# Attention: values of heads 0 to 3 as plain fp32 products of copied weights and values instead of three products of rounded and low parts

## The chip, the cores and the metric

The kernel runs on one core of one Trainium2 chip. The metric is the device time of an execution in microseconds (us). A core has a matrix engine (TensorE, in profiles PE for the products and PEld for the loads of their stationary operand), three engines for elementwise work (VectorE or DVE, ScalarE or ACT, GpSimd or POOL) and SyncE (SP), which issues the DMA transfers here. Operands of TensorE lie in SBUF, its results in PSUM. Each engine works through its own list of instructions in order and waits on semaphores for the others.

## The reference

The reference is a small diffusion transformer of two layers, in fp32: 256 latent and 256 context tokens of width 1024. Each layer has a half feed-forward block, a mixer, and another half feed-forward block, each with its modulation, residual and layer norm. The mixer of the first layer is attention with 8 query heads on 2 key-value heads of width 128; that of the second is an mLSTM. What the change touches is the attention's softmax and its product with the values:

```python
def gqa_softmax(q, k, v):
    s = jnp.einsum('bqhgd,bkhd->bhgqk', q, k).astype(jnp.float32) * (ATT_HEAD_DIM ** -0.5)
    p = jax.nn.softmax(s, axis=-1).astype(v.dtype)
    return jnp.einsum('bhgqk,bkhd->bqhgd', p, v)
...
    ob = lax.map(lambda qblk: gqa_softmax(qblk, k_all, v_all), qb)
...
        oc = gqa_softmax(qc.reshape(B, Lc, ATT_KV_HEADS, ATT_GROUP, ATT_HEAD_DIM), kc, vc)
```

Latent queries see all 512 tokens, context queries the 256 context tokens. Heads 0 to 3 use key-value head 0, heads 4 to 7 key-value head 1.

## The kernel before

All activations stand transposed in SBUF: 8 tiles of 128 features by 512 tokens, the latent tokens in columns 0 to 255, the context in 256 to 511. A product of fp32 operands is made as three products of type fp32r: `split` (L224) writes a rounded copy `h` with ScalarE (L225) and the low part `x - h` with VectorE (L230), and `mm3` (L239) adds up high × high, high × low and low × high in PSUM (all three on L241). Weights come in chunks of 128×1024 through `raw` (L204, the DMA on SyncE) and are split likewise.

Attention (L947) first makes keys, values and queries: `part` makes one token tile (128 tokens) of one block of 256 columns with `token_product` (L935, products on L941 to L943); `evac` (L971) takes the results out of PSUM, `turn` (L990) transposes queries and keys on TensorE (L998) and applies the rotation. For block 0, `evac` splits the values (L978) into `vt`, a rounded and a low tile of 4 token tiles × 2 key-value heads × 128.

Then the loop of L1143 runs over 24 steps, head by head, three steps `i` a head. Steps 0 and 1 are the two blocks of 128 latent queries against all 512 tokens, step 2 holds both blocks of context queries against the 256 context tokens. `scores` (L1024) makes the 128×512 scores in three rounded products, or six of half the width in step 2, and its softmax: minimum (the scores are negated) on VectorE (L1036), exponential with its sum on ScalarE (L1039), reciprocal (L1043), scaling (L1049, on POOL for step 0, on VectorE else). Three steps later (`AHEAD`) `values` (L1052) transposes the weights on TensorE (L1056) into one of two PSUM tiles (`ps`, L200), and splits that tile: steps 0 and 1 into the halves of `pT` (L1064), step 2 into `pC` (L1066). In step 2 it then makes the head's output: four groups of three rounded products for the latent columns (L1068) and two groups for the context columns (L1072), each 128×256. The output is split into the input of the out projection (L1078), or for head 0, while a projection still uses that place, copied to `qT` (L1080). `queries` (L1019) splits the next head's queries.

Between these stand the projections that are left (`rest`, L1132), the loads of the output weights (`OUTAT`), and from step 20 on the first half of the out projection (`mix_unit`, L1158). The order of the instructions of each engine isn't the order of the code: a list scheduler sets it from its own costs, unless an instruction is held in program order by `pin` (the transposes are, L998 and L1056).

Of the kernel before, what the change touches and what calls it, by code (L numbers as in the profile page):

```python
# [9 lines left out]
F32 = mybir.dt.float32  # L10
F32R = mybir.dt.float32r
# [7 lines left out]
P = 128  # L19
D = 1024  # L20
ND = D // P
T = 512
TL = 256
# [8 lines left out]
BLOCK = 64  # L32

SH = 16
SHM = 48
# [137 lines left out]
class Body:  # L173
# [12 lines left out]
    def t(self, shape, dt=F32, tag=None, bufs=None, pool=None):  # L186
        self.n += 1
        kw = {"bufs": bufs} if bufs else {}
        return (pool or self.sp).tile(list(shape), dt, name=f"t{self.n}", tag=tag or f"u{self.n}", **kw)
# [757 lines left out]
    def attention(self, gate, side):  # L947
        nc, V, S, a = self.nc, self.nc.vector, self.nc.scalar, self.a
        with self.tc.tile_pool(name="att", bufs=1) as gp:
            t = lambda shape, dt=F32, **k: self.t(shape, dt, pool=gp, **k)  # L950
# [5 lines left out]
            for tab, g in zip(tabs, (gq, gk)):  # L956
                S.activation(tab, tabs[1], AF.Copy, scale=g)
            qT = t([P, HEADS, T])
            kT, vt = ([t(shape, F32R) for _ in range(2)] for shape in ([P, 2, T], [P, 4, 2, P]))
            acc, ws = {}, {}  # L960

            def part(blk, tt, step=lambda k: None, ks=range(ND)):
# [8 lines left out]
            def evac(blk, tts):  # L971

                n = 4 if blk else 2
                ss = self.small(len(tts) * n)
                os = [acc[blk, tt].rearrange("p (n f) -> p n f", f=P) for tt in tts]
                for j, (tt, o) in enumerate(zip(tts, os)):
                    if not blk:
                        self.split(o[:, 2:4, :], vt[0][:, tt], vt[1][:, tt])  # L978
                    sq = self.tmp(n * P).rearrange("p (n f) -> p n f", f=P)
                    S.activation(sq, o[:, :n, :], AF.Square)  # L980
                    V.tensor_reduce(ss[:, j * n : (j + 1) * n], sq, AX.X, ALU.add)
                r = self.rsqrt(ss, len(tts) * n, RMS_EPS, 1.0 / P)
                qs = [t([P, n, P], tag="qn", bufs=3) for _ in tts]
                for i in range(n):
                    for j, (q, o) in enumerate(zip(qs, os)):
                        S.activation(q[:, i, :], o[:, i, :], AF.Copy, scale=r[:, j * n + i : j * n + i + 1])
                m = 4 // len(tts)
                return [lambda i=i: turn(blk, tts, i, min(m, n - i), qs) for i in range(0, n, m)]
# [63 lines left out]
            def values(hd, i, e, pt):  # L1052
                kv = hd // 4
                tp = self.ps()
                for k in range(4):
                    self.pin(nc.tensor.transpose(tp[:, k * P : (k + 1) * P], e[:, k * P : (k + 1) * P], self.ident))  # L1056
                if i == 0:
                    pt[:] = [
                        [x.rearrange("p (k q f) -> p k q f", k=4, q=2) for x in self.pair(sh=SHM)],
                        [t([P, 4 * P + BLOCK], F32R, tag=k, bufs=2)[:, SHM : SHM + 4 * P].rearrange("p (k q f) -> p k q f", k=2, q=2) for k in ("ph", "pl")],  # L1060
                    ]
                pT, pC = pt
                if i < 2:
                    self.split(tp.rearrange("p (k f) -> p k f", f=P), *(x[:, :, i, :] for x in pT))  # L1064
                    return
                self.split(tp.rearrange("p (q k f) -> p k q f", q=2, k=2), *pC)  # L1066
                o = self.mm()
                for k in range(4):  # L1068
                    self.mm3(
                        o[:, 0:TL], [x[:, k, kv, :] for x in vt], [x[:, k].rearrange("p q f -> p (q f)") for x in pT], k == 0, k == 3  # L1070
                    )
                for k in range(2):  # L1072
                    self.mm3(
                        o[:, TL:T], [x[:, 2 + k, kv, :] for x in vt], [x[:, k].rearrange("p q f -> p (q f)") for x in pC],
                        k == 0, k == 1,
                    )
                if (2, 3) in acc:
                    self.split(o, self.xh[:, hd, :T], self.xl[:, hd, :T])  # L1078
                else:
                    S.copy(qT[:, hd, :], o)  # L1080
                    kept.append(hd)
# [9 lines left out]
            def done(n, blk, tts, lag=LAG):  # L1091
                wait.extend((n + lag + i, f) for i, f in enumerate(evac(blk, tts)))

            n = 0
# [47 lines left out]
            es, pt = [], []  # L1142
            for n in range(max(len(subs) + AHEAD, MIXAT + ND)):  # L1143
                if n < len(subs):
                    hd, i = subs[n]
# [623 lines left out]
```

## Time and profile before

| what | value |
|---|---|
| time, median of 3 runs | 1627.38 us (1626.02 to 1630.14) |
| span of the profiled execution, first to last instruction | 1625.5 us |
| mean granted TensorE clock | 0.997 |
| attention heads, start of the first and of the last transpose of weights | 451.3 and 525.3 us |
| bytes by DMA, mean rate | 251.56 MB, 155 GB/s |

The span is the only time recorded of the profiled execution itself; it lies 1.9 us under the median. Times in the timeline are counted from the start of the span. A group's line gives line, engine, operation, output and inputs, shapes, count, then busy time, mean duration in ns, and the idle time of the engine ahead of these instructions with what ended it. In the timeline a row has start and duration in us, engine, line, operation, shapes and count of merged instructions, and in brackets the idle time of that engine before it, with the instruction that ended it. PE shows a plain fp32 product as two records. A matmul's shown duration is longer than the distance to the next one, since matmuls are pipelined; the distance between starts is what one costs.

### The profile page before, as it was taken

The page shows a single profiled execution, that of the slowest core. Times are in us where ns is not written, and L with a number is a line of the kernel's source. Part 1 is how long each engine was busy: PE and PEld are TensorE (multiplying, and loading weights), DVE is VectorE, ACT ScalarE, POOL GpSimd, SP SyncE. Part 2 cuts the span into 40 slices and gives each one's busy share as a digit, 9 for nine tenths or more (in the row PEclk, how much of TensorE's full clock was granted, in tenths as well). Part 3 has the DMA queues.
Part 4 walks back from the last instruction along what each step waited for, and adds up shares of the span by engine and source line. Part 5 has one row for each costly group of instructions (what it writes and reads, how often), then busy time and mean ns, then how long its engine had stood idle before and what let it go on. Part 6 is the DMA issues. An engine that isn't in the chain of part 4 may idle for free. (4 is left out here: it accounts for less than half of the span.)

```text
span 1625.5 us, 26587 instructions
## 1 busy us (share of the span) xinstructions
PE 1606.9 (99%) x10304; PEld 1451.7 (89%) x10304; DVE 1355.7 (83%) x2699; ACT 749.2 (46%) x1272; POOL 63.0 (4%) x77
## 2 busy tenths in 40 slices
PE   9999999999999999999999999999999999999998
PEld 7888888889988998889998998889999989999987
DVE  7899977649889879899986879699966968897687
ACT  6522132314676443316652444336652657566542
POOL 0000000001011100000000100000001000030000
PEclk9999999999999999999999999999999999999999
DMA  9687766422202447633445258713363343437552
GB/s 358 221 252 237 235 205 187 137 66 85 66 1 80 151 134 221 219 117 105 129 146 180 79 165 289 253 58 118 104 225 100 98 130 87 142 110 253 181 176 91
DMA packets 72222, 251.56 MB, mean 155 GB/s; under 512 B 7960, under 2 KB 10776, under 8 KB 72096
## 3 DMA queue, kind: packets, MB, share of 16 engines
q1 hardware_dynamic: 71520, 249.09, 47.7%
q8 instruction: 80, 1.31, 0.3%
q10 hardware_dynamic: 576, 0.79, 0.1%
q14 instruction: 46, 0.38, 0.1%
HBM read 248.79 MB, written 1.05 MB: 154 GB/s over the span
## 5 line engine op out<-in xcount | busy, mean ns | idle before, releaser
L241 PE MATMUL t<-t,t 128*128 128x256 f32 (+2 forms) x8412 | 1317.0, 318 | 6.4 <-ACT t L225 3.3
L241 PEld LDWEIGHTS t<-t,t 128*128 128x128 f32 x8412 | 1185.7, 188 | 125.4 <-ACT t L225 4.7
L225 ACT CAST t<-t 128x1024 fp32r<-128x1024 f32 (+3 forms) x521 | 428.5, 844 | 485.8 <-PE t L241 214.5
L230 DVE TENSOR_TENSOR t<-t,t 128x256 fp32r<-128x256 f32 (+2 forms) x740 | 513.8, 729 | 111.9 <-ACT t L225 107.7
L350 DVE SCALAR_TENSOR_TENSOR t<-t,t 128x1024 bf16<-128x1024 f32 x224 | 260.7, 1220 | 0.0
L588 ACT ACTIVATE t<-t 128x512 f32<-128x512 f32 (+1 forms) x71 | 34.5, 490 | 103.5 <-PE t L241 102.4
L941 PE MATMUL t<-t,t 128*128 128x256 f32 (+1 forms) x256 | 79.3, 310 | 0.0
L718 DVE SCALAR_TENSOR_TENSOR t<-t,t,t 128x256 f32<-128x256 f32 x96 | 42.7, 478 | 43.9 <-PE t L241 43.7
L943 PE MATMUL t<-t,t 128*128 128x256 f32 (+1 forms) x256 | 78.4, 306 | 0.0
L942 PE MATMUL t<-t,t 128*128 128x256 f32 (+1 forms) x256 | 78.4, 306 | 0.0
L589 DVE TENSOR_TENSOR t<-t,t 128x512 f32<-128x512 f32 (+1 forms) x71 | 39.0, 553 | 40.6 <-PE t L241 28.1
L484 POOL TENSOR_TENSOR t<-t,t 128x256 f32<-128x256 f32 x30 | 23.4, 781 | 1104.9 <-ACT t L474 1103.5
L869 PE MATMUL t<-t,t 128*128 128x512 f32 (+1 forms) x300 | 60.5, 364 | 0.0
L869 PEld LDWEIGHTS t<-t,t 128*128 128x128 f32 x300 | 51.5, 189 | 8.9
L474 ACT ACTIVATE t<-t 128x256 f32<-128x256 f32 x72 | 26.1, 412 | 65.5 <-DVE t L467 65.5
L1456 PE MATMUL t<-t,t 128*128 128x512 f32 (+2 forms) x276 | 55.6, 356 | 0.0
L1456 PEld LDWEIGHTS t<-t,t 128*128 128x128 f32 (+1 forms) x276 | 44.9, 183 | 10.9 <-issue 0.9
L942 PEld LDWEIGHTS t<-t,t 128*128 128x128 f32 x256 | 48.1, 188 | 3.0 <-DVE t L230 0.5
L941 PEld LDWEIGHTS t<-t,t 128*128 128x128 f32 x256 | 48.3, 189 | 2.7
L943 PEld LDWEIGHTS t<-t,t 128*128 128x128 f32 x256 | 48.1, 188 | 2.5
L541 ACT ACTIVATE t<-t,t 128x256 fp32r<-128x256 f32 x72 | 32.8, 503 | 30.1 <-DVE t L540 30.1
L641 DVE TENSOR_TENSOR t<-t,t 128x512 f32<-128x512 f32 x66 | 45.2, 685 | 0.4
(206 smaller groups left out, 1078.6 us busy)
## 6 DMA issues: line engine op xcount, KB each, us to landing
t<-in_ffn_in SPq DMA_DIRECT2D x168, 512.0 KB, 4.1
t<-in_ada_w SPq DMA_DIRECT2D x138, 512.0 KB, 4.4
t<-in_ffn_out SPq DMA_DIRECT2D x66, 512.0 KB, 4.5
t<-in_ffn_last SPq DMA_DIRECT2D x22, 512.0 KB, 3.5
t<-in_att_in SPq DMA_DIRECT2D x12, 512.0 KB, 3.5
t<-in_att_out SPq DMA_DIRECT2D x8, 512.0 KB, 3.6
t<-in_ml_qk SPq DMA_DIRECT2D x8, 512.0 KB, 3.6
t<-in_ml_v SPq DMA_DIRECT2D x8, 512.0 KB, 3.5
```

What stands on the lines that cost most here:

```text
L225: self.behind(self.nc.scalar.copy(h, x))
L230: self.behind(self.nc.vector.tensor_tensor(out=ls, in0=xs, in1=hs.bitcast(F32), op=ALU.subtract))
L241: mm = lambda *k, **kw: self.nc.tensor.matmul(*k, skip_group_check=not group, **kw)
L350: ins = nc.vector.scalar_tensor_tensor(self.tmp().bitcast(BF16), r, 1.0, self.cb[:, v, :], ALU.mult, ALU.mult, accum_out=to)
L589: V.tensor_tensor(out=sl, in0=sl, in1=pu[:, :n], op=ALU.mult)
L641: add = lambda o, x, y: V.tensor_tensor(out=o, in0=x, in1=y, op=ALU.add)
L718: V.scalar_tensor_tensor(z, y[:, gg[0] - t0 : gg[1] - t0], gate()[:, v, d : d + 1], z, ALU.mult, ALU.add)
L869: pin(nc.tensor.matmul(o, gs[g], ws[k][w][:, i : i + n], start=k == k0 and g == w == 0, stop=k == k1 - 1 and g == 1,))
L941: mm(o, self.xh[:, k, c], wh, start=k == 0, stop=False)
L942: mm(o, self.xh[:, k, c], wl, start=False, stop=False)
L943: mm(o, self.xl[:, k, c], wh, start=False, stop=k == ND - 1)
L1456: mm = lambda *k, **kw: pin(nc.tensor.matmul(*k, **kw))
```

## The change

Only attention is changed. For key-value head 0, `evac` copies the values unrounded into `vf`, and `values` copies the transposed weights unrounded (on ScalarE, into a buffer of the same ring `w`, without the offset of 48 columns, and for the context into a new tile `pf` with two buffers) and makes one plain fp32 product for each group of three. `vt` keeps key-value head 1 alone. For heads 4 to 7 the computation is that of before.

```diff
-            kT, vt = ([t(shape, F32R) for _ in range(2)] for shape in ([P, 2, T], [P, 4, 2, P]))
+            kT, vt = ([t(shape, F32R) for _ in range(2)] for shape in ([P, 2, T], [P, 4, P]))
+            vf = t([P, 4, P])
...
                     if not blk:
-                        self.split(o[:, 2:4, :], vt[0][:, tt], vt[1][:, tt])
+                        S.copy(vf[:, tt], o[:, 2, :])
+                        self.split(o[:, 3, :], vt[0][:, tt], vt[1][:, tt])
...
+                if not kv:
+                    if i == 0:
+                        x, y = self.pair(F32)[0], t([P, 4 * P], tag="pf", bufs=2)
+                        pt[:] = [x.rearrange("p (k q f) -> p k q f", k=4, q=2), y.rearrange("p (k q f) -> p k q f", k=2, q=2)]
+                    if i < 2:
+                        S.copy(pt[0][:, :, i, :], tp.rearrange("p (k f) -> p k f", f=P))
+                        return
+                    S.copy(pt[1], tp.rearrange("p (q k f) -> p k q f", q=2, k=2))
+                    o = self.mm()
+                    for x, c, n in ((pt[0], 0, 4), (pt[1], TL, 2)):
+                        for k in range(n):
+                            nc.tensor.matmul(
+                                o[:, c : c + TL], vf[:, 4 - n + k, :], x[:, k].rearrange("p q f -> p (q f)"), start=k == 0, stop=k == n - 1
+                            )
+                else:
...
+                    for c, ps, n in ((0, pT, 4), (TL, pC, 2)):
+                        for k in range(n):
+                            self.mm3(
+                                o[:, c : c + TL], [x[:, 4 - n + k, :] for x in vt], [x[:, k].rearrange("p q f -> p (q f)") for x in ps],
+                                k == 0, k == n - 1,
+                            )
```

The scheduler orders the stage anew. Three places follow, as the rows of the instruction lists before and after. The new code stands 2 to 14 lines lower: transposes of weights are L1058 there, the plain products L1070, the minimum L1038, the reciprocal L1045.

TensorE in head 0, before: `t_4183` are scores of step 2, `t_4176` takes the transposed weights of step 1, `t_4207` is the head's output, `t_3106` and `t_3107` are rounded and low values and `t_4144` the weights of steps 0 and 1.

```order
L241 MATMUL t_4183<-t_3104,t_4023 128x256
L241 MATMUL t_4183<-t_3105,t_4023 128x256
L241 MATMUL t_4183<-t_3104,t_4024 128x256
L1056 MATMUL t_4176<-t_69,t_4035 128x128 x4
L241 MATMUL t_4207<-t_4144,t_3106 128x256 x2
L241 MATMUL t_4207<-t_4144,t_3107 128x256
L241 MATMUL t_4207<-t_4144,t_3106 128x256 x2
L241 MATMUL t_4207<-t_4144,t_3107 128x256
```

The same place after: `t_4179` takes the transposed weights of step 1, `t_4185` are the scores of step 2, `t_4208` is the output, `t_4149` the copied weights and `t_3108` the copied values.

```order
L1058 MATMUL t_4179<-t_69,t_4040 128x128 x4
L241 MATMUL t_4185<-t_3104,t_4028 128x256
L241 MATMUL t_4185<-t_3105,t_4028 128x256
L241 MATMUL t_4185<-t_3104,t_4029 128x256
L241 MATMUL t_4185<-t_3104,t_4028 128x256
L241 MATMUL t_4185<-t_3105,t_4028 128x256
L241 MATMUL t_4185<-t_3104,t_4029 128x256
L1070 MATMUL t_4208<-t_4149,t_3108 128x256 x4
L241 MATMUL t_4222<-t_3104,t_4163 128x512
```

The transposes moved ahead of six score products, which now stand between them and the first product with the values; twelve rounded products became four plain ones.

VectorE at the same time, before: `t_4144` on L230 is the low part of the weights of steps 0 and 1, `t_4161` and `t_4256` are low parts of queries, `t_4117` is the minimum of the scores of step 2, and L261 to L268 are the root of `rsqrt` for a block of queries.

```order
L230 TENSOR_TENSOR t_4161<-t_3103,t_4160 128x512
L254 TENSOR_SCALAR t_4092<-t_4088 128x4
L230 TENSOR_TENSOR t_4144<-t_4139,t_4144 128x4x128
L261 TENSOR_SCALAR t_4094<-t_4092 128x4
L262 SCALAR_TENSOR_TENSOR t_4095<-t_4094 128x4
L263 TENSOR_TENSOR t_4095<-t_4095,t_4092 128x4
L230 TENSOR_TENSOR t_4256<-t_3103,t_4255 128x512
L264 SCALAR_TENSOR_TENSOR t_4096<-t_4095 128x4
L1036 TENSOR_REDUCE t_4117<-t_4110 128x2
L265 SCALAR_TENSOR_TENSOR t_4094<-t_4096,t_4094 128x4
L230 TENSOR_TENSOR t_4144<-t_4176,t_4144 128x4x128
```

And after, with `t_4122` as that minimum and `t_4243` as the low part of the queries:

```order
L230 TENSOR_TENSOR t_4164<-t_3103,t_4163 128x512
L254 TENSOR_SCALAR t_4097<-t_4093 128x4
L261 TENSOR_SCALAR t_4099<-t_4097 128x4
L262 SCALAR_TENSOR_TENSOR t_4100<-t_4099 128x4
L263 TENSOR_TENSOR t_4100<-t_4100,t_4097 128x4
L264 SCALAR_TENSOR_TENSOR t_4101<-t_4100 128x4
L1038 TENSOR_REDUCE t_4122<-t_4115 128x2
L265 SCALAR_TENSOR_TENSOR t_4099<-t_4101,t_4099 128x4
L266 TENSOR_TENSOR t_4100<-t_4099 128x4
L230 TENSOR_TENSOR t_4243<-t_3103,t_4242 128x512
```

Both low parts of the weights are gone from the list, and the minimum stands ahead of the second queries' low part.

TensorE in head 3, before: `t_4541` takes the transposed weights of step 1, `t_4565` those of step 2, `t_4572` is the output, `t_4593` and `t_4619` are scores two heads on.

```order
L1056 MATMUL t_4541<-t_69,t_4436 128x128 x4
L241 MATMUL t_4572<-t_4509,t_3106 128x256
L241 MATMUL t_4593<-t_3104,t_4525 128x512
L241 MATMUL t_4593<-t_3105,t_4525 128x512
L241 MATMUL t_4593<-t_3104,t_4526 128x512
L241 MATMUL t_4619<-t_3104,t_4525 128x512
L1056 MATMUL t_4565<-t_69,t_4458 128x128 x4
```

And after: `t_4519` takes the transposed weights of step 2, `t_4525` is the output, `t_4466` are the weights of steps 0 and 1, `t_4467` those of step 2, `t_4534` scores of head 5, `t_4546` the transposed weights of head 4, step 0.

```order
L1058 MATMUL t_4519<-t_69,t_4428 128x128 x4
L1070 MATMUL t_4525<-t_4466,t_3108 128x256 x4
L1070 MATMUL t_4525<-t_4467,t_3108 128x256 x2
L241 MATMUL t_4534<-t_3104,t_4480 128x512
L241 MATMUL t_4534<-t_3105,t_4480 128x512
L241 MATMUL t_4534<-t_3104,t_4481 128x512
L1058 MATMUL t_4546<-t_69,t_4457 128x128 x4
```

All six products of the head now stand in one block behind its last transposes, where before the first of them stood directly behind the transposes of step 1 and the rest after those of step 2. Heads 1 and 2 have the same block. POOL and SP issue the same number of instructions as before.

More of the change, by code (lines that the diff above doesn't have):

```diff
@@ L1056, in values @@
                     self.pin(nc.tensor.transpose(tp[:, k * P : (k + 1) * P], e[:, k * P : (k + 1) * P], self.ident))
[L1057 to L1076, printed above, removed]
+                if not kv:
[13 more added lines that the diff above has]
+                else:
+                    if i == 0:
+                        pt[:] = [
+                            [x.rearrange("p (k q f) -> p k q f", k=4, q=2) for x in self.pair(sh=SHM)],
+                            [t([P, 4 * P + BLOCK], F32R, tag=k, bufs=2)[:, SHM : SHM + 4 * P].rearrange("p (k q f) -> p k q f", k=2, q=2) for k in ("ph", "pl")],
+                        ]
+                    pT, pC = pt
+                    if i < 2:
+                        self.split(tp.rearrange("p (k f) -> p k f", f=P), *(x[:, :, i, :] for x in pT))
+                        return
+                    self.split(tp.rearrange("p (q k f) -> p k q f", q=2, k=2), *pC)
+                    o = self.mm()
+                    for c, ps, n in ((0, pT, 4), (TL, pC, 2)):
[4 more added lines that the diff above has]
+                            )
```

## The prediction

> **What bounds the kernel now.** First the page's busy shares, then the time by stage, then the order of instructions inside the one stage that the change touches.
>
> ```profile
> span 1625.5 us, 26587 instructions
> PE 1606.9 (99%) x10304; PEld 1451.7 (89%) x10304; DVE 1355.7 (83%) x2699; ACT 749.2 (46%) x1272; POOL 63.0 (4%) x77
> ```
>
> TensorE is busy for 99% of the span, so nearly everywhere a microsecond more of matmul work is a microsecond more of time. The profiled execution spans 1625.5 us, 1.9 us under the median of the runs, 1627.38; I work out a difference and put it on both. What another engine's relief can be worth is limited to the places where TensorE stands still. The next view gives the stretches around the attention heads: length, then busy time of PE, PEld, DVE, ACT and POOL with its count, the granted clock, the share of DMA and GB/s.
>
> ```profile
> 400.00:446.00 46.00, 46.00 (x398) 45.37 (x396) 39.70 (x98) 31.23 (x71) 0.00 (x0) 1.00 0.20 60
> ...
> 456.40:460.00 3.60, 3.60 (x17) 3.42 (x18) 3.46 (x10) 2.11 (x8) 1.01 (x1) 0.53 0.00 0
> ...
> 505.00:530.00 25.00, 24.82 (x153) 21.81 (x152) 21.92 (x47) 14.30 (x24) 1.57 (x1) 1.00 0.37 121
> ```
> ```profile
> 451.00:490.00 39.00, 35.46 (x247) 31.85 (x246) 35.02 (x88) 26.56 (x70) 6.27 (x4) 0.96 0.01 1
> 490.00:505.00 15.00, 12.16 (x81) 10.58 (x80) 13.87 (x29) 10.84 (x26) 3.14 (x2) 1.00 0.18 46
> ```
>
> From 400 to 446 TensorE never waits, and from 505 hardly at all. Between 451 and 505 it does: 3.5 of 39 us while heads 0 to 3 run, 2.8 of 15 us in heads 4 and 5. There VectorE is as loaded as TensorE (35.0 of 39, 13.9 of 15 us), so this stage hangs on the interplay of the two. The third view is the order of time, with the idle time ahead of a row in brackets. Head 0 first:
>
> ```profile
> 453.55 0.60 PE L1056 MATMUL t<-t,t 128*128 128x128 f32 x4
> ...
> 454.28 0.69 DVE L230 TENSOR_TENSOR t<-t,t 128x512 fp32r<-128x512 f32 x1 [0.44 <-ACT t L225]
> ...
> 454.82 0.38 PE L241 MATMUL t<-t,t 128*128 128x256 f32 x1 [0.68 <-ACT t L225]
> 454.89 0.15 DVE L264 SCALAR_TENSOR_TENSOR t<-t 128x4 f32<-128x4 f32 x1
> 454.96 0.68 DVE L1036 TENSOR_REDUCE t<-t 128x2 f32<-128x512 f32 x1
> 455.56 0.15 DVE L265 SCALAR_TENSOR_TENSOR t<-t,t 128x4 f32<-128x4 f32 x1
> 455.63 0.68 DVE L230 TENSOR_TENSOR t<-t,t 128x512 fp32r<-128x512 f32 x1
> ...
> 456.37 3.05 PE L241 MATMUL t<-t,t 128*128 128x256 f32 x12 [1.16 <-DVE t L230]
> ```
>
> The transposes of the weights end at 454.15. The value product waits 0.68 us for ScalarE's rounded copy, then 1.16 us more for VectorE's low part, which stood behind a maximum, a query's low part and two steps of a root. Right behind these two gaps the granted clock is 0.53 for 3.6 us (456.4 to 460, the row above): 3.6 × 0.47 = 1.7 us more. The other stops that belong here:
>
> ```profile
> 476.66 0.65 PE L1056 MATMUL t<-t,t 128*128 128x128 f32 x4 [0.20 <-ACT t L1013]
> ...
> 477.66 0.53 PEld L241 LDWEIGHTS t<-t,t 128*128 128x128 f32 x3 [0.33 <-ACT t L225]
> ```
> ```profile
> 483.54 0.63 PE L1056 MATMUL t<-t,t 128*128 128x128 f32 x4 [0.63 <-DVE t L230]
> ...
> 484.84 1.29 PE L241 MATMUL t<-t,t 128*128 128x256 f32 x5 [0.68 <-ACT t L225]
> ...
> 492.40 0.62 PE L241 MATMUL t<-t,t 128*128 128x256 f32 x2 [1.77 <-ACT t L225]
> ```
> ```profile
> 499.29 0.66 PE L1056 MATMUL t<-t,t 128*128 128x128 f32 x4 [1.06 <-DVE t L230]
> ```
>
> 483.54 and 499.29 are transposes that wait for VectorE because its low part still reads the PSUM tile (two buffers) that they write next. The brackets understate the loss: a 256-column product is shown 0.28 us long, while its successor starts 0.114 us after it (rows below), so each bracket hides about 0.165 us. The six large gaps are 0.68 + 1.16 + 0.63 + 0.68 + 1.77 + 1.06 = 5.98, with 6 × 0.165 about 7.0 us; the two small ones about 0.7, the clock 1.7. **The pool is 9.4 us**; nothing else in the program can pay for this change.
>
> **The change part by part.** *Products.* 24 groups of three rounded products (six for each of four heads) become 24 plain fp32 products of the same shape. The trace has plain fp32 products of this shape at L1282, four calls in a row, which show as eight records; the three-product price is read from ten neighbours:
>
> ```profile
> 1339.08 1.71 PEld L1282 LDWEIGHTS t<-t,t 128*128 128x128 f32 x8
> 1340.81 0.19 PEld L1292 LDWEIGHTS t<-t,t 128*128 128x128 f32 x1
> ```
> ```profile
> 467.58 0.28 PE L943 MATMUL t<-t,t 128*128 128x256 f32 x1
> ...
> 468.72 0.87 PE L241 MATMUL t<-t,t 128*128 128x256 f32 x6
> ```
>
> (1340.81 − 1339.08) / 4 = 0.4325 us a call; (468.72 − 467.58) / 10 = 0.114 us a rounded product, three of them 0.342. So each group costs 0.0905 us more, 24 of them **+2.2 us**, on the path, since TensorE has no slack. The operands now start at another offset in their buffers; no row shows that for fp32, and I take nothing for it. [...]
>
> *Weights' copies.* Twelve casts on ScalarE become twelve copies of the same size; twelve subtractions on VectorE go.
>
> ```profile
> L230 DVE TENSOR_TENSOR t<-t,t 128x512 fp32r<-128x512 f32 x38 | 25.6, 684 | 3.4 <-ACT t L225 3.1
> ...
> L225 ACT CAST t<-t 128x512 fp32r<-128x512 f32 x38 | 21.9, 597 | 16.3 <-PE t L1056 10.3 <-PE t L241 5.9
> ...
> L1080 ACT COPY t<-t 128x512 f32<-128x512 f32 x1 | 0.6, 588 | 0.5 <-PE t L241 0.5
> ```
>
> ScalarE: 588 for 597 ns, nothing. VectorE: 12 × 0.684 = 8.2 us less in the 39 us of heads 0 to 3, from 35.0 to 26.8, while TensorE's own work rises. So there VectorE stops being a bound, the value products wait for one ScalarE copy and no longer for a chain of two engines, and the PSUM tiles of the transposes come free at the copy.
>
> *Values' copies.* Once per token tile, a 256-wide cast and subtraction become a 128-wide copy, cast and subtraction.
>
> ```profile
> L225 ACT CAST t<-t 128x256 fp32r<-128x256 f32 x58 | 22.8, 401 | 17.6 <-DVE t L589 9.6 <-PE t L943 3.7 <-PE t L241 2.0
> ...
> L986 ACT ACTIVATE t<-t,t 128x128 f32<-128x128 f32 x40 | 11.2, 378 | 5.3 <-DVE t L268 4.0 <-PE t L998 1.2
> ...
> L225 ACT CAST t<-t 128x128 fp32r<-128x128 f32 x8 | 2.4, 294 | 0.0
> ```
>
> For the new copy 294 to 378 ns bound it; I take the cast's 294: 4 × (2 × 294 − 401) = +0.75 us on ScalarE (at most +1.1), spread over two places before 446. The projections hide it: TensorE is busy 46.00 of 46 us from 400 to 446 and ScalarE 31. Without that cover it would cost those 0.75 to 1.1 us. No wait is added and no DMA issue: SP and POOL keep their instructions.
>
> *What the moved order recovers.* By the rows in the part on the change: in head 0 the transposes of the second block now stand ahead of six score products (6 × 0.114 = 0.7 us) and the value products behind these, so of the first gap (0.68 + 0.165) 0.7 goes, the second (1.16 + 0.165) goes with the low part, and if the gaps go, so does the clock's fall: 0.7 + 1.3 + 1.7 = **3.7**. In heads 1 to 3 the last transposes are followed by four products of older weights, 4 × 0.4325 = 1.7 us, which cover the 0.59 us copy that the other two need; head 3's gaps (0.63 + 0.68 + 0.33) go: **1.6**. Of the small steps of 476 to 478, half: **0.4**. Heads 4 and 5 keep rounded and low parts. VectorE reaches them without arrears, but its load from 490 to 505 is still 13.9 of 15 us; of 1.77 + 1.06 + 0.33 = 3.2 I take half, between none and all: **1.6**. What is late next is ScalarE's cast for the first product of heads 4 and 5.
>
> Sum: +2.2 − 3.7 − 1.6 − 0.4 − 1.6 = **−5.1 us**: span 1620.4, median **1622.3**. After 505 the saving is kept, as that stretch is full of matmuls and its loads are issued when buffers come free, so they move with it.
>
> **The rivals.**
> *All of the pool goes* (9.4 − 2.2 = −7.2, 1620.2): for it, ScalarE (26.6 of 39 us) and VectorE (26.8) both have room; against it, heads 4 and 5 don't change in kind.
> *Only head 0 is relieved* (−3.7 + 2.2, 1625.9): five of the eight gaps name ScalarE, whose copies stay; then gaps re-form at the copy in heads 1 to 3.
> *The clock falls all the same* (−5.1 + 1.7, 1624.0): for it, its cause is only inferred from two gaps of 0.7 and 1.2 us ahead of it; the larger gap at 492 has no fall behind it. [...]
> *Nothing is recovered* (1629.5): the dearer products replace the waits one for one.
> *Slower.* The six products hold TensorE 2.6 us in a row, with the next head's scores queued behind them. These scores must pass maximum, exponential, reciprocal and a scaling on POOL before their transposes:
>
> ```profile
> L1049 POOL TENSOR_SCALAR t<-t,t 128x512 f32<-128x512 f32 x8 | 12.5, 1568 | 105.4 <-DVE t L1043 96.1 <-PE t L241 9.3
> ...
> L1039 ACT ACTIVATE t<-t,t 128x512 f32<-128x512 f32 x16 | 11.2, 700 | 3.2 <-DVE t L1036 3.2
> L1036 DVE TENSOR_REDUCE t<-t 128x1 f32<-128x512 f32 x16 | 10.8, 676 | 0.1
> ```
>
> That is 0.68 + 0.70 + 1.57, about 3.3 us with the small steps. If a queue makes it longer than the work between scores and transposes (about 6.5 us in the new order: three other score groups, transposes and the 2.6 us block), each head would stop for about a microsecond: +2.2 + 4 = 1633.6 with the old gaps kept. It decides only from 3 us of delay on; a chance of 5%.
> *The products aren't what they are said to be*: were each one pass, 24 × (0.114 − 0.342) = −5.5 instead of +2.2, 1614.6; L1282 shows two records a call, so 1%.
>
> **How the numbers follow.** Forecast 0.38, all of the pool 0.25, clock falls 0.09, head 0 only 0.14, nothing 0.08, slower 0.05, one pass 0.01. A measurement of this kernel tells about 0.3% (4.9 us) from no change, so faster means under 1622.5. All of the pool, one pass and a little over half of the forecast's own spread (1621 to 1624) lie there: 0.47. Slower means over 1632.3: 0.06 with the tail of the case in which nothing is recovered; within, 0.47. The range takes in all but the ends: down to 1618.5, the whole pool with 1.7 us for gaps too small to be listed, up to 1629.5.
>
> **What would show it.** In the new profile: 48 records of the plain products, a fresh pair every 0.43 us (else the +2.2 is wrong); VectorE about 8 us less busy over heads 0 to 3; no bracket over 0.3 us on TensorE between the first transposes and the end of head 3 (else the order, or ScalarE's copy, is the limit); granted clock 1.00 throughout them; in heads 4 and 5 a remaining gap of 1 to 2 us that names ScalarE's cast. The prediction is wrong if gaps re-form in heads 1 to 3, if the clock falls elsewhere, or if the stretch behind the heads starts earlier but is no longer full.

## The result, and the profile after

The changed kernel takes **1625.21 us** (median of 16 runs, 1623.99 to 1626.67) against 1628.00 us for the kernel before in the same runs (1625.74 to 1630.14): ratio 0.9983, 95% interval 0.9976 to 0.9989, which is 2.8 us less (1.8 to 3.9). The forecast of 1622.3 us was 5.1 us below 1627.38. The sign is right, about half of the gain came. The difference is 0.17% of the time, less than the runs of the kernel before spread among themselves (1625.74 to 1630.14); only the medians tell the two kernels apart.

The head of the page after, and the stretches around the heads (length, then busy time of PE, PEld, DVE, ACT and POOL, granted clock, DMA share, GB/s):

```profile
span 1622.9 us, 26548 instructions
...
PE 1608.2 (99%) x10280; PEld 1450.3 (89%) x10280; DVE 1349.3 (83%) x2687; ACT 749.0 (46%) x1276; POOL 62.4 (4%) x77
```
```profile
400.00:446.00 46.00, 45.66 (x390) 44.73 (x389) 38.80 (x95) 30.64 (x73) 0.00 (x0) 1.00 0.20 58
451.90:485.80 33.90, 33.41 (x209) 28.68 (x208) 27.66 (x74) 25.30 (x67) 6.26 (x4) 1.00 0.00 1
485.80:501.00 15.20, 14.12 (x94) 12.33 (x93) 14.67 (x33) 11.72 (x30) 3.13 (x2) 1.00 0.22 59
```

In heads 0 to 3 (second row) TensorE now stands still for 0.5 of 33.9 us, VectorE is busy for 27.7 of them, where it was for 35.0 of the 39 us from 451 to 490, and the clock stays at 1.00. Ahead of the heads (first row) TensorE no longer works through: 45.66 of 46 us, where it was 46.00. TensorE's order of time in the heads, with the idle time ahead of a row and its releaser in brackets:

```profile
454.81 1.99 PE L1070 MATMUL t<-t,t 128*128 128x256 f32 x8
...
468.07 2.76 PE L1070 MATMUL t<-t,t 128*128 128x256 f32 x12
...
482.04 0.66 PE L1058 MATMUL t<-t,t 128*128 128x128 f32 x4 [0.24 <-ACT t L1064]
482.53 2.76 PE L1070 MATMUL t<-t,t 128*128 128x256 f32 x12
...
488.46 1.07 PE L241 MATMUL t<-t,t 128*128 128x256 f32 x4 [0.20 <-ACT t L225]
...
495.77 5.26 PE L241 MATMUL t<-t,t 128*128 128x256 f32 x28 [0.73 <-ACT t L225]
```

Six plain products (twelve records) take 2.76 us; without the 0.16 us by which the last record is shown longer than its step, that is 0.433 us each, as forecast. Through head 3 no bracket is over 0.24 us; what remains is 0.20 and 0.73 us in heads 4 and 5, where 1.77 and 1.06 stood.

One measure carries the rest of this study: the stretch from the first to the last transposes of weights, heads 0 to 7. The bounds of each window row are those two starts. The kernel before, then the changed one:

```profile
451.30:525.30 74.00, 67.63 (x440) 59.74 (x439) 66.10 (x151) 48.22 (x115) 10.97 (x7) 0.98 0.13 38
```
```profile
452.00:521.30 69.30, 67.74 (x416) 58.45 (x415) 59.48 (x139) 48.05 (x115) 10.96 (x7) 1.00 0.14 40
```

74.0 us became 69.3: the heads gain 4.7 us, close to the 5.1 of the forecast. An estimate splits this: at the distances from start to start that the traces show where nothing waits (0.109 us for a transpose, 0.114 and 0.227 us for a rounded product of 256 and 512 columns, 0.216 us for a plain record), the matmuls of the stretch come to about 62.0 us before and 64.2 after. So the products cost 2.2 us more and 6.9 us of other time went (12.0 to 5.1); the forecast had +2.2 and −7.3. So the question is twofold: why only 2.8 us of 4.7 arrive at the end, and whether the two terms are what the forecast took them for.

### The profile page after: what moved, and what is told of

Read it like the earlier page. It is cut to its first block, busy times and chain, and to the rows that moved or that the text cites. A ratio compares the mean times of both kernels' runs of the same rounds, so it can differ in the third digit from the quotient of the medians.

```text
span 1622.9 us, 26548 instructions
## 1 busy us (share of the span) xinstructions
PE 1608.2 (99%) x10280; PEld 1450.3 (89%) x10280; DVE 1349.3 (83%) x2687; ACT 749.0 (46%) x1276; POOL 62.4 (4%) x77
## 5 line engine op out<-in xcount | busy, mean ns | idle before, releaser
L225 ACT CAST t<-t 128x1024 fp32r<-128x1024 f32 (+3 forms) x509 | 421.6, 850 | 479.3 <-PE t L241 225.0
L230 DVE TENSOR_TENSOR t<-t,t 128x256 fp32r<-128x256 f32 (+2 forms) x728 | 505.4, 729 | 110.7 <-ACT t L225 106.9
L589 DVE TENSOR_TENSOR t<-t,t 128x512 f32<-128x512 f32 (+1 forms) x71 | 39.0, 553 | 40.6 <-PE t L241 27.7
L474 ACT ACTIVATE t<-t 128x256 f32<-128x256 f32 x72 | 26.1, 412 | 65.8 <-DVE t L467 65.8
L942 PEld LDWEIGHTS t<-t,t 128*128 128x128 f32 x256 | 48.1, 188 | 3.3 <-DVE t L230 0.8
L943 PEld LDWEIGHTS t<-t,t 128*128 128x128 f32 x256 | 48.1, 188 | 2.8 <-DVE t L542 0.3
```

The source lines that it names most:

```text
L225: self.behind(self.nc.scalar.copy(h, x))
L230: self.behind(self.nc.vector.tensor_tensor(out=ls, in0=xs, in1=hs.bitcast(F32), op=ALU.subtract))
L589: V.tensor_tensor(out=sl, in0=sl, in1=pu[:, :n], op=ALU.mult)
L942: mm(o, self.xh[:, k, c], wl, start=False, stop=False)
L943: mm(o, self.xl[:, k, c], wh, start=False, stop=k == ND - 1)
```

## The experiments

Each kernel was timed against the kernel before, on the same chip and in turns. Where a gain or a loss up to some point is given, it is the difference of the starts of matching TensorE instructions against the first profile of the kernel before. Every edit makes the scheduler order the stage anew, so a few tenths of a microsecond between two kernels can be order alone.

| kernel | median, us (before) | ratio, interval | heads' stretch, us | VectorE busy in it | TensorE busy in it |
|---|---|---|---|---|---|
| before, first, second and third profile | 1628.15 (1628.32) for the second | 1.0003 [0.9994, 1.0011] | 74.0; 73.0; 74.1 | 66.1; 65.9; 66.1 | 67.6; 66.6; 67.7 |
| changed | 1625.21 (1628.00) | 0.9983 [0.9976, 0.9989] | 69.3 | 59.5 | 67.7 |
| changed, again | 1625.39 (1627.87) | 0.9983 [0.9974, 0.9992] | 69.3 | 59.6 | 67.8 |
| VectorE's subtractions put back | 1627.46 (1627.87) | 0.9995 [0.9986, 1.0004] | 72.3 | 65.8 | 68.1 |
| one rounded product | 1625.46 (1627.87) | 0.9984 [0.9975, 0.9993] | 69.7 | 58.8 | 62.6 |
| three rounded, no subtraction | 1625.33 (1627.95) | 0.9982 [0.9973, 0.9990] | 70.1 | 59.7 | 65.9 |
| head 0 alone | 1627.72 (1627.95) | 0.9999 [0.9990, 1.0007] | 72.1 | 64.3 | 67.2 |
| heads 1 to 3 alone | 1625.71 (1627.95) | 0.9988 [0.9979, 0.9996] | 70.2 | 61.0 | 67.1 |
| heads 0 to 5 | 1625.28 (1628.32) | 0.9982 [0.9973, 0.9991] | 69.6 | 56.7 | 68.4 |
| values added on POOL | 1624.71 (1627.87) | 0.9980 [0.9971, 0.9989] | 69.3 | 59.6 | 67.7 |
| values copied on VectorE | 1625.65 (1627.95) | 0.9985 [0.9976, 0.9993] | 69.3 | 59.6 | 67.8 |
| values added late on VectorE | 1624.18 (1628.54) | 0.9977 [0.9967, 0.9987] | 69.3 | 59.6 | 67.7 |

### What the heads' gain is made of

My theory was the forecast's: VectorE's relief pays, and the dearer products are paid on the path. The rival: the pace of the heads is set by the chain of scores, maximum, exponential, scaling, transposes and copies on VectorE and ScalarE, and TensorE's price lies beside it.

**The subtractions put back.** The twelve low parts are computed again, into a tile that nobody reads:

```diff
+                        V.tensor_tensor(out=lo, in0=tp.rearrange("p (k f) -> p k f", f=P), in1=pt[0][:, :, i, :], op=ALU.subtract)
...
```

> The changed kernel with the twelve subtractions of VectorE put back: the low parts of the weights of heads 0 to 3 are computed into a tile that nothing reads. TensorE's work is that of the changed kernel. Theory: VectorE's relief (12 x 0.68 = 8.2 us, and the earlier release of the transposes' tiles) pays for most of the recovered waits; but the products no longer wait for the low part, so only a part comes back: waits on TensorE in the heads of 5.2 us rise to 8 or 9, the time is 3 to 4 us over the changed kernel, that is within 1 us of the kernel before. Rival: the waits went because the products wait for one copy alone and the order changed; then the time stays within 1 us of the changed kernel.

**One rounded product.** `vf`, the copied weights and `pf` become `F32R` tiles, so heads 0 to 3 make one rounded product of rounded operands and no low parts:

```diff
-            vf = t([P, 4, P])
+            vf = t([P, 4, P], F32R)
...
-                        x, y = self.pair(F32)[0], t([P, 4 * P], tag="pf", bufs=2)
+                        x, y = self.pair()[0], t([P, 4 * P], F32R, tag="pf", bufs=2)
```

> Weights and values of heads 0 to 3 are rounded only, and one rounded product takes the place of the plain fp32 one: the low parts are left out, so the output is less exact. Theory: the price of a plain product is on TensorE's path, 0.4325 against 0.114 us, 24 of them: 7.6 us under the changed kernel if no new wait takes their place, and 5 to 6 if VectorE (28 us in the heads 0 to 3) or ScalarE then set the pace. Rival: the heads are no longer bound by TensorE, and the products' price is hidden: less than 3 us under the changed kernel.

**Three rounded products, no subtraction.** The kernel before, but in heads 0 to 3 the low part of the weights is left out: ScalarE's rounded copy stands in its place, so the three products keep their number and length and the output is no longer that of the reference:

```diff
                 pT, pC = pt
+                if not kv:
+                    pT, pC = [pT[0], pT[0]], [pC[0], pC[0]]
+                if i < 2 and not kv:
+                    S.copy(pT[0][:, :, i, :], tp.rearrange("p (k f) -> p k f", f=P))
+                    return
...
```

> The kernel before, except that in heads 0 to 3 ScalarE rounds the transposed weights and VectorE's 12 subtractions are left out: the rounded weights stand in for their low part, so the three products a block keep their number and length. TensorE's work is that of before (no price), VectorE's relief is that of the change, and everything ahead of the heads keeps its order. My sum's way (relief 6.9 us and price 2.2 us both on the path): the heads gain 6.5 to 7 us, ratio 0.9955 to 0.9962. The rival (score chain on VectorE and ScalarE sets the pace once VectorE is relieved, and the longer products lie beside it): the heads gain 4.3 to 5.0 us as in the changed kernel, ratio 0.9968 to 0.9976.

The same window row for the three, in this order:

```profile
452.40:524.70 72.30, 68.08 (x416) 58.37 (x415) 65.78 (x151) 48.12 (x115) 10.95 (x7) 1.00 0.13 39
```
```profile
453.00:522.70 69.70, 62.60 (x391) 53.66 (x390) 58.81 (x139) 48.12 (x115) 10.95 (x7) 0.98 0.14 40
```
```profile
451.20:521.30 70.10, 65.88 (x441) 57.92 (x439) 59.67 (x139) 48.16 (x115) 10.95 (x7) 1.00 0.13 41
```

With the subtractions back, 3.0 us of the heads' gain are lost again; TensorE's work is that of the changed kernel. The time is 2.1 us over the changed kernel's 1625.39 in the same runs, less than the 3 to 4 that I expected, and within 1 us of the kernel before. The products with the values don't read the low part here and wait for ScalarE's copy alone, as the first of them shows:

```profile
455.92 2.00 PE L1072 MATMUL t<-t,t 128*128 128x256 f32 x8 [0.67 <-ACT t L1064]
```

So what these 3.0 us are paid for is VectorE's work and the PSUM tiles of the transposes, which the subtraction reads too (between 451 and 506 the transposes wait for it once, 0.2 us). The run puts back both together, and no run separates them. With VectorE's relief kept, as in the other two kernels, TensorE's busy time falls by 2 us (three rounded) or 5 us (one rounded), and the stretch does not become shorter: 70.1 and 69.7 against 69.3. What TensorE saves it stands still instead, as its rows show, in the kernel with one rounded product and in that with three:

```profile
486.21 0.66 PE L1058 MATMUL t<-t,t 128*128 128x128 f32 x4 [1.14 <-DVE t L1051]
...
496.68 0.41 PE L1058 MATMUL t<-t,t 128*128 128x128 f32 x2 [1.75 <-DVE t L1051]
```
```profile
475.73 3.10 PE L241 MATMUL t<-t,t 128*128 128x256 f32 x21 [1.00 <-ACT t L1066]
...
495.22 0.66 PE L1056 MATMUL t<-t,t 128*128 128x128 f32 x4 [2.15 <-DVE t L230]
```

My theory fell here, and the rival held in kind: VectorE's relief makes the gain, the price of the plain products is hidden. The heads of the kernel with three rounded products gain 3.9 us, a little less than the 4.3 to 5.0 that the rival expected and far from my 6.5 to 7. One reservation belongs to the kernel with one product: its clock fell behind the gap at 486.2 (0.50 for 3.41 us), a loss of up to 1.7 us; without it the stretch might be 68 us, which is still only 1.3 of 5 us. Its runs also spread more than those of the other versions (1622.14 to 1628.90 us). The kernel with three products has the clock at 1.00 and no such reservation.

**Head 0 alone, heads 1 to 3 alone.** The condition becomes `hd == 0` or `0 < hd < 4`; rounded, low and plain values are all kept, with the copy on VectorE.

```diff
-                if not kv:
+                if hd == 0:
...
```

> Only head 0 with plain products; heads 1 to 3 as before (rounded and low parts of the values are kept beside the copy, which VectorE makes). My steps: head 0's two gaps and the fall of the clock go, 3.7 us, price 0.5 us: the heads gain 3 to 3.4 us, ratio 0.998. Rival (what counts is VectorE's work in the whole stretch): three of twelve subtractions gone are a quarter of 4.7 us: the heads gain 1.0 to 1.5 us, ratio 0.9991 to 0.9995.

> The other part of the change: heads 1 to 3 with plain products, head 0 as before (three rounded products). My steps: the waits of head 0 and the fall of the clock stay, 1.6 + 0.4 + 1.6 us of later waits go, price 1.6 us: the heads gain 2 us, ratio 0.9985 to 0.999, and the granted clock near 458 is again 0.5 to 0.6 for some microseconds. Rival (VectorE's work in the whole stretch): three quarters of 4.7 us, the heads gain 3.2 to 3.8 us, ratio 0.9975 to 0.998.

```profile
451.40:523.50 72.10, 67.24 (x434) 58.29 (x433) 64.34 (x148) 48.10 (x115) 10.95 (x7) 1.00 0.13 39
```
```profile
452.50:522.70 70.20, 67.05 (x421) 58.58 (x420) 60.96 (x142) 47.87 (x115) 10.96 (x7) 1.00 0.12 40
```

Heads 1 to 3 alone gain 3.8 us of the 4.7, three quarters and a little more, and not the 2.0 of my steps. Head 0 alone gains 1.9 us, between the two expectations. It had gained 2.5 us at 470, when its own gaps had gone, and 1.9 us at 505: head 1's chain gave part of it back. A gap that was removed in one head was not kept in full while the next heads' chain stayed as it was. What counts, by these two kernels, is VectorE's work in the whole stretch. In the whole time head 0 alone gains nothing (ratio 0.9999): it loses 0.6 us ahead of the heads, where the values are copied on VectorE, and the rest in small steps behind them.

**Heads 0 to 5.** The condition becomes `hd < 6`, and `vf` holds both groups' values, copied on VectorE.

> Plain products in heads 0 to 5 (both groups' values copied on VectorE, rounded and low parts kept for the second group alone, for heads 6 and 7). Theory (VectorE and ScalarE's chain sets the pace of the heads as long as TensorE waits in them, the longer products lie beside it): the waits of the changed kernel's heads 4 and 5, 2.0 us in the trace, mostly go, the price of 12 longer products, 1.1 us, is hidden: 1 to 2 us below the changed kernel, ratio 0.9972 to 0.9978. Rival (in heads 4 and 5 TensorE has less slack and the price is paid, or the chain is ScalarE's, which makes as many copies as before): within 0.5 us of the changed kernel, ratio 0.998 to 0.9986.

```profile
452.30:521.90 69.60, 68.39 (x404) 58.73 (x403) 56.74 (x133) 47.82 (x115) 10.95 (x7) 1.00 0.12 40
```

VectorE has 2.7 us less to do than in the changed kernel, and nothing is won; the rival held. TensorE is busy 68.4 of 69.6 us, so it is the limit here; its largest stop names ScalarE's copy:

```profile
495.78 2.00 PE L1070 MATMUL t<-t,t 128*128 128x256 f32 x8 [0.70 <-ACT t L1064]
```

So the changed kernel stands where the limits meet: relief of VectorE beyond its 59.5 us gained nothing, as TensorE was full then, and relief of TensorE alone gained nothing, as the chain on VectorE and ScalarE then sets the length though neither of the two is full (58.8 and 48.1 of 69.7 us with one rounded product).

### The fall of the clock

**The kernel before, a second and a third time.** No edit.

> The kernel before, unchanged, timed against itself and profiled a second time. Theory (part of the 4.7 us that the heads gain from one trace to the other is the fall of the granted clock to 0.53 near 458 in the first profile, which not every execution has: kernels with gaps of 0.84 and 1.33 us at the same place showed 1.00): the heads are 1.5 to 1.9 us shorter here than in the first profile with no clock under 0.9 between 452 and 468, and the step of 0.4 us near 1488 that every kernel showed against the first profile is in this one too. Rival (the fall belongs to this kernel's gaps): the clock falls again near 458, the heads take 74 us from the first transposes to the last. Ratio 0.9992 to 1.0008 by both.

> The kernel before a third time, for its trace alone. As for the second: by the theory the heads are 1.5 to 1.9 us shorter than in the first profile in some executions, with no fall of the clock near 458; by the rival they take 74 us with the clock near 0.53 for some 3 us in each.

The second profile has the same gap, no fall behind it (the granted clock is the third number from the end), and a stretch one microsecond shorter:

```profile
456.20 1.79 PE L241 MATMUL t<-t,t 128*128 128x256 f32 x12 [1.16 <-DVE t L230]
```
```profile
458.00:460.00 2.00, 2.00 (x14) 1.69 (x13) 1.91 (x4) 1.04 (x3) 1.18 (x1) 1.00 0.00 0
...
451.10:524.10 73.00, 66.59 (x440) 58.44 (x439) 65.94 (x151) 47.95 (x115) 10.97 (x7) 1.00 0.13 38
```

The third has the fall again, and 74.1 us from 451.2 to 525.3:

```profile
458.00:460.00 2.00, 2.00 (x11) 1.82 (x10) 1.91 (x4) 0.58 (x2) 1.05 (x1) 0.50 0.00 0
```

Neither expectation holds for both: the fall comes in two of three profiles of one kernel. Right behind it, at 460, the second profile is 1.6 us further ahead of the first than at 450; 0.5 of that is gone by 480, and 1.0 is left at the end of the heads, not 1.7. The kernel with plain products in heads 1 to 3 alone has the gaps of head 0 too, without a fall:

```profile
457.64 1.81 PE L241 MATMUL t<-t,t 128*128 128x256 f32 x12 [1.16 <-DVE t L230]
```
```profile
458.00:460.00 2.00, 2.00 (x18) 1.93 (x17) 1.95 (x7) 1.89 (x7) 0.00 (x0) 1.00 0.00 0
```

The traces say more on when it falls. In the first profile the clock changes between 1.00 and 0.50 at 456.49, 459.91 and 1620.44, points that lie 1 and 340 steps of 3.413 us apart. So time can be cut into such steps, and the busy time of TensorE (first after the length) read step by step. In the first profile of the kernel before the step ahead of the fall, the fall, and the step with the gap of 1.77 us:

```profile
453.08:456.49 3.41, 1.57 (x12) 1.14 (x11) 2.86 (x11) 1.96 (x5) 0.00 (x0) 1.00 0.01 2
456.49:459.90 3.41, 3.41 (x16) 3.23 (x17) 3.28 (x10) 2.02 (x8) 0.91 (x1) 0.50 0.00 0
...
490.63:494.04 3.41, 1.64 (x10) 1.43 (x11) 2.65 (x6) 2.26 (x7) 1.57 (x1) 1.00 0.00 0
```

In the second profile, with the steps counted back from the fall at the kernel's end (1622.66 us), a border at 455.30 lies inside head 0's second gap, so the idle time is shared by two steps:

```profile
451.88:455.30 3.42, 2.48 (x17) 1.91 (x15) 2.85 (x9) 1.58 (x3) 0.00 (x0) 1.00 0.01 2
455.30:458.71 3.41, 2.51 (x18) 2.42 (x19) 3.27 (x13) 3.08 (x11) 0.00 (x0) 1.00 0.00 0
```

And the kernel with one rounded product, ahead of its fall and in it:

```profile
484.98:488.39 3.41, 1.60 (x9) 1.18 (x9) 3.38 (x9) 2.85 (x8) 0.00 (x0) 1.00 0.00 0
488.39:491.80 3.41, 3.41 (x14) 2.92 (x14) 2.14 (x6) 1.71 (x5) 1.56 (x1) 0.50 0.00 0
```

In these rows the clock fell behind the steps in which TensorE was busy for 1.57 and 1.60 of 3.41 us, and 1.58 in the third profile, and not behind those with 1.64, 2.48 and 2.51. With both gaps of head 0 in one step it fell (first and third profile), with the gaps shared by two steps it did not (second). The product behind the second gap starts at 456.37 in the first profile and at 456.20 in the second, and the border near it lies at 456.49 and at 455.30. For the kernel with heads 1 to 3 alone no row here shows where its borders lie. One fall does not fit: the profile of the last kernel below has one from 1431.73 to 1435.14, behind a step with 3.12 us of busy time, and why that one came is open.

Against the profile without a fall, the heads of the changed kernel gain 73.0 − 69.3 = 3.7 us; head 0 alone 0.9 and heads 1 to 3 alone 2.8, which add up to it and stand as one to three, like their subtractions.

### What is lost outside the heads

**The changed kernel again.** No edit.

> The changed kernel once more, for a second profile. Theory: its gain lies in the heads (TensorE's clockwise lead there moved from +0.7 to -4.0 us in the first profile), 0.9 us are lost where queries of the first token tiles are taken out (405 to 408 us), and the further 1.4 us lost after 1440 us are chance (waits for weights): the lead behind the heads is again -4.0, but the losses after 1440 us fall elsewhere or differ. Rival: the late losses come from the shift itself; then the second profile shows the same steps of +0.4 near 1445 and +0.9 near 1602 us. Time about 2.8 us under the kernel before in either case.

In the two profiles of the changed kernel TensorE loses 0.6 and 0.9 us to the kernel before between 360 and 440, ahead of the heads. The chain is read on ScalarE and VectorE, after (ScalarE, then VectorE):

```profile
401.05 0.51 ACT L541 ACTIVATE t<-t,t 128x256 fp32r<-128x256 f32 x1 [3.44 <-DVE t L540]
401.46 1.12 ACT L988 ACTIVATE t<-t,t 128x128 f32<-128x128 f32 x4
402.46 0.52 ACT L541 ACTIVATE t<-t,t 128x256 fp32r<-128x256 f32 x1
```
```profile
403.02 0.48 DVE L542 SCALAR_TENSOR_TENSOR t<-t,t,t 128x256 fp32r<-128x256 f32 x1 [0.94 <-ACT t L541]
```

and before (the same two engines):

```profile
400.95 0.97 ACT L541 ACTIVATE t<-t,t 128x256 fp32r<-128x256 f32 x2 [3.19 <-DVE t L540]
```
```profile
401.97 0.48 DVE L542 SCALAR_TENSOR_TENSOR t<-t,t,t 128x256 fp32r<-128x256 f32 x1
```

With the values' copies in `evac` the scheduler puts four scalings of queries and keys (1.12 us) between the first and the second step of the context's norm; VectorE waits 0.94 us for the second, and the norm's six further tiles and the projections that read them come that much later. TensorE stops twice, at 406.9 and 407.5, where two starts lie 0.37 and 0.30 us further apart than the 0.114 us of such a product; the row of the first:

```profile
406.86 0.39 PE L941 MATMUL t<-t,t 128*128 128x256 f32 x1 [0.21 <-ACT t L541]
```

Three places for the values were tried.

**Added on POOL** (rounded plus low part, `evac` as before) and **copied on VectorE**:

```diff
+            nc.gpsimd.tensor_tensor(out=vf, in0=vt[0][:, :, 0, :].bitcast(F32), in1=vt[1][:, :, 0, :].bitcast(F32), op=ALU.add)
```

> Values of both key-value heads are split as before, and the plain values are added up from rounded and low part on POOL just ahead of the heads, so the taking out of block 0 has the same instructions and order as before the change; the heads are those of the changed kernel. Theory: the step of +0.86 us at 405 to 408 us is gone and the heads keep their -4.7 us, so the lead behind the heads is -4.8 and the time about 0.9 us under the changed kernel (3.5 to 4 under the kernel before). Rival: the step comes from elsewhere, or the heads lose as much by waiting for POOL (one addition, 1 to 2 us, ahead of the first product): then the time is that of the changed kernel.

```diff
-                        S.copy(vf[:, tt], o[:, 2, :])
+                        V.tensor_copy(vf[:, tt], o[:, 2, :])
```

> The changed kernel with the four copies of the values on VectorE instead of ScalarE. Theory (the copies on ScalarE put four scalings ahead of the context norm's step and cost TensorE 0.7 to 1.0 us near 406): that loss is gone, the heads keep their gain of 4.7 us, about 0.9 us below the changed kernel, ratio 0.9976 to 0.9980. Rival (any copy at that place delays the same norm, VectorE's as much as ScalarE's): the loss of 0.7 to 1.0 us stays, ratio 0.9983 as the changed kernel.

The stops near 407 are gone with POOL, and shorter with VectorE's copy (0.40 us), but both kernels lose as much a little later: 0.9 and 1.1 us between 360 and 440. With POOL 0.8 of the loss comes near 423, and it is VectorE's, in the kernel with the addition on POOL (both engines) and in the kernel before:

```profile
417.37 1.91 DVE L563 SCALAR_TENSOR_TENSOR t<-t,t,t 128x256 f32<-128x256 f32 x2
...
417.53 1.47 POOL L1154 TENSOR_TENSOR t<-t,t 128x512 f32<-128x512 f32 x1 [24.25 <-DVE t L230]
```
```profile
417.30 0.87 DVE L563 SCALAR_TENSOR_TENSOR t<-t,t,t 128x256 f32<-128x256 f32 x2
```

Two VectorE instructions that take 0.87 us last 1.91 us beside POOL's addition, in front of the root that the keys' transposes wait for. Neither theory held as I had put it: the loss came with either engine, so I take it that the copies' place among the norms is the point and not their engine.

**Added late on VectorE.** `evac` as before; one addition, tied behind the minimum of head 0's second block:

```diff
+                if (hd, i) == (0, 1):
+                    ins = V.tensor_tensor(out=vf, in0=vt[0][:, :, 0, :].bitcast(F32), in1=vt[1][:, :, 0, :].bitcast(F32), op=ALU.add)
+                    edge = mybir.DependencyInfo(mybir.DependencyClass.NoSync, mybir.DependencyReason.DATA)
+                    self.tc.add_manual_dep(ins.ins, red.ins.name, edge, reason="behind the scores")
```

> The changed kernel with the plain values made late: the values leave the accumulator as before (one cast and one subtraction for both groups), and VectorE adds rounded and low parts of the first group once, behind the score minimum of head 0's second block, where it stood idle for 2 us in the kernel before. Theory (every kernel with plain values so far lost 0.6 to 1.3 us to the kernel before between 360 and 440, since the copies or the addition stood among the norms' work): ahead of the heads TensorE stands within 0.3 us of the kernel before, the heads keep 4.4 to 4.8 us against its first profile, and the whole is 0.7 to 1 us below the changed kernel, ratio 0.9974 to 0.9979. Rival (what is won ahead of the heads is waited for again in them or later): ratio 0.9981 to 0.9986, as the changed kernel.

VectorE's order of time, then the stretch ahead of the heads and the heads:

```profile
447.73 0.83 DVE L1039 TENSOR_TENSOR t<-t,t 128x512 f32<-128x512 f32 x1
449.81 0.16 DVE L1048 RECIPROCAL t<-t 128x1 f32<-128x1 f32 x1 [1.25 <-ACT t L1044]
```
```profile
400.00:446.00 46.00, 46.00 (x397) 45.37 (x396) 39.69 (x97) 31.29 (x71) 0.00 (x0) 1.00 0.18 59
...
450.30:519.60 69.30, 67.74 (x415) 58.43 (x414) 59.56 (x139) 48.05 (x115) 10.96 (x7) 1.00 0.13 40
```

The addition stands where VectorE was idle and still leaves 1.25 us idle behind it. TensorE works through again (46.00 of 46), starts the heads 1.7 us earlier than the changed kernel (0.5 us of it was there at 360 already), and keeps their length. This version takes 1624.18 us, 4.4 us below the kernel before (ratio 0.9977, 0.9967 to 0.9987), as the theory had it (0.9974 to 0.9979). Its profile is 5.7 us ahead of the kernel before at the end of the heads and loses 1.5 of that at the fall of the clock at 1431.73. By time alone it is not told from the changed kernel (0.9983), as the intervals overlap; that the loss ahead of the heads is gone is shown by the trace.

## Why the prediction was right, and where it was wrong

- **Where the kernel can gain.** Right: the gain lies between 451 and 505, it comes out of TensorE's waits there, and the chain of two engines in head 0 went with the low parts.
- **Products, +2.2 us "on the path, since TensorE has no slack".** The size is right (0.433 us a product, against 0.114 for a rounded one), the place wrong. With 2 and 5 us less of TensorE's work the heads' length stayed at 70.1 and 69.7 us. In the sum this did no harm: without the price the same time would have stood there as waits, as these two kernels show, so a price that was not on the path and waits that were not all to be had cancelled. That is luck.
- **Weights' copies.** Right, and most of the gain: the subtractions put back take 3.0 us, out of 3.7 where neither kernel has a fall of the clock. VectorE's busy time in the stretch fell by 6.6 us, not by 8.2: in a row its instructions start sooner than their shown length (454.28 and 454.89 in head 0 before, 0.61 us apart for 0.69).
- **Values' copies "hidden by the projections".** This is the step that failed, with 0.6 and 0.9 us in the two profiles against nothing in the sum. That TensorE was busy for 46.00 of 46 us said that nothing was late there, not that there was room: the norms' chain had none to spare, and the scheduler put other work into it. The forecast looked for the moved order in the heads only.
- **Head 0, 3.7 us.** The two gaps went. The clock's fall was put into the sum at 1.7 us as a part of every execution; it cost 1.0 us at the end of the heads and came in two of three profiles. It came behind the two gaps where both lay in one step of 3.41 us (1.57 and 1.58 us busy) and not where two steps shared them (2.48 and 2.51), which agrees with the two gaps as its cause; the rival in which the clock falls all the same came in neither profile of the changed kernel. And the sum by places does not hold: alone, head 0 gains 1.9 us (0.9 against the profile without a fall), not the 3.7 less its price of 0.5.
- **Heads 3, 4 and 5.** Right in kind: no bracket over 0.24 us in head 3, and the remaining stops in heads 4 and 5 name ScalarE's cast, with 0.2 and 0.7 us, less than the 1 to 2 us expected. With the hidden 0.165 us each, 3.2 us of stops there became 1.3, so 1.9 went where 1.6 was forecast.
- **The rival that was slower.** A block of six products holds TensorE 2.76 us, and the next heads' transposes wait 0.24 us at most behind it; it does not decide.
- **The saving "is kept".** Mostly. The lead at the end of the heads was 4.0 and 3.3 us in the two profiles, at the end 2.6 and 2.3. Of the loss 0.4 us near 1449 belongs to the first profile of the kernel before, which is that much quicker there than its other two; the rest came at places that differ from run to run, and no cause was looked for.

Put together: of the forecast's 5.1 us the heads give 4.7 where the clock falls and 3.7 where it doesn't; 0.6 to 0.9 us are lost ahead of them. That leaves 2.8 to 4.1 ahead of the losses behind the heads, and 2.8 (1.8 to 3.9) was measured. That the heads' 4.7 came so near to 5.1 is in part luck: 1.0 of it is the fall of the clock in the profile that it is measured against.

## What to carry to other kernels

In a stage like this one, where two engines were busy for 67.6 and 66.1 of 74.0 us, vary one engine's work at a time before its price or relief is put into a sum: here 2 and 5 us less work on TensorE left the stage at 70.1 and 69.7 us, against 69.3, while putting 6.3 us back on VectorE cost 3.0 us, and taking a further 2.7 us off it gained nothing, with TensorE busy for 68.4 of 69.6 us. A few tenths of a microsecond of new work were not free ahead of the heads (0.6 and 0.9 us lost), where TensorE had been busy for 46.00 of 46 us: what counts is whether the chain that they are put into has room, which the busy share of another engine does not show; tie such work to a place where its engine is seen to be idle. A loss that is seen in one profile, such as a fall of the clock, is worth its price times the share of executions that have it; a second and a third profile of the unchanged kernel tell that share.

## What the runs showed of the hardware

- **VectorE's instructions took longer beside one of POOL.** Two three-operand VectorE instructions on 128x256 took 1.91 us beside POOL's addition of 1.47 us, and 0.87 us without it; the profile shows longer instructions and no wait. By the kernel's code two of the operands that each VectorE instruction reads lie in SBUF, and so do POOL's. What makes the 1.04 us more, no run shows.
- **In the heads the clock fell behind idle time added up over a step of 3.41 us, not behind the longest single gap.** With the same gaps of 0.68 and 1.16 us on TensorE, the granted clock fell to 0.50 for 3.41 us in two of three profiles of one kernel: where TensorE was busy for 1.57 and 1.58 us of one step, and not where the gaps were shared by two steps (2.48 and 2.51 us busy). A step with 1.60 us had a fall behind it; one with 1.64 us, which holds the heads' longest gap in the first profile (1.77 us), had none; and one fall, behind a step with 3.12 us, stays unexplained. Why the clock falls, and at how much idle time, no run shows.
